# Split weights kept in DRAM after the first token block: one paired load in place of a load, a cast and a subtraction

## The chip, the cores and the metric

The kernel runs on one core of a Trainium2 chip. The metric is the device time of one execution in microseconds (us). Engines: PE (TensorE; PEld is its weight load), DVE (VectorE), ACT (ScalarE), POOL (GpSimd) and SP (SyncE), which here issues every DMA. All DMAs of the core run on the same 16 DMA engines.

## The reference

One decoder layer on x of 2048 tokens by 1024 channels, in float32:

```python
h = _rmsnorm(x, norm_w[l])
proj = h @ w_in[l]                      # 1024 x 8456 columns
(a_q, a_f, a_i, a_g, b_qkv, b_z, b_beta, b_a,
 c_q, c_k, c_v, c_g, gate_logits) = jnp.split(proj, split_points, axis=-1)
y_a = _hgrn2_branch(...)                # gated linear recurrence, 4 heads
y_b = _gated_deltanet_branch(...)       # delta rule, 4 heads
y_c = _swa_sink_branch(...)             # sliding-window attention
ys = jnp.stack([y_a, y_b, y_c], axis=2)
lifted = jnp.einsum('bsnc,ncd->bsnd', ys, w_branch[l])
merged = jnp.sum(jax.nn.sigmoid(gate_logits...) * lifted, axis=2)
x = x + merged @ w_out[l]
return _rmsnorm(x, final_norm)
```

## The kernel before

The 2048 tokens are worked off in four blocks of 512 (`block(s)`). Each block runs through all the weights once: the projections of channel-major outputs (`wct`, through `proj_ct`), of token-major ones (`wtc`, through `proj_v`), the lifts (`wb`, through `merge`) and the output projection (`wo`, through `output`).

To get float32 precision out of products in the type float32r, each matrix is used as a high and a low part, and each product is three matmuls: high by high, high by low, low by high (lines 80 to 82 and 148 to 150). `load_w` (lines 62 to 70) brings one weight tile of 128 partitions by up to 512 columns: a DMA on SP into `wraw` (256 KB; 162 KB for the 324 columns of `wtc`), a cast on ACT into `wh` (line 68) and a subtraction on DVE into `wl` (line 69). A block uses 178 tiles, and `load_w` is called anew for each in each block, 712 times in all. A tile of 512 columns feeds 12 matmuls of 512 columns.

`wraw`, `wh` and `wl` have `WB` = 4 buffers each. So up to four raw tiles can lie loaded and up to four split ones can lie ready; `wraw` becomes free when the subtraction has read it, `wh` and `wl` when the PE has read them.

Beside the projections, `unit_a`, `unit_b` and `unit_c` do the three branches head by head, in chains of small matmuls and of DVE, ACT and POOL work. `unit_b` passes through DRAM several times, one DMA after another: lines 536 (`scrN<-NS`), 539 (`L<-scrN`), 547 (`scrX<-L`) and 549 (`XB<-scrX`). In the first block `bias_c` also writes a table of 1.5 MB (line 261, `scr<-rw`) and reads it back (line 263). The start, ahead of the first block, makes the `wtc` products from the raw input while x is still arriving (`start`, line 178).

In the last block, the second half of `output` calls `mm_tc` with `step` 4: four tiles at a time are held, and each group of four output rows goes through all four before the next row group.

The order of the instructions on each engine and queue is not that of the source: a planner sets it when the program is built, and each queue then works in that fixed order. `tc.issue_after` ties two places to an order by hand.

Of the kernel before, what the change touches and what calls it, by code (L numbers as in the profile page):

```python
# [11 lines left out]
F32 = mybir.dt.float32  # L12
F32R = mybir.dt.float32r
# [3 lines left out]
ALU = mybir.AluOpType  # L17
# [3 lines left out]
P = 128  # L21
# [10 lines left out]
WB = 4  # L32
# [6 lines left out]
def _trunk(tc, S, a, out):  # L39
    nc = tc.nc  # L40
# [4 lines left out]
    sb = ctx.enter_context(tc.tile_pool(name="sb", bufs=2))  # L45
    ps = ctx.enter_context(tc.tile_pool(name="ps", bufs=4, space=PSUM))
    dram = ctx.enter_context(tc.tile_pool(name="dram", bufs=1, space=DRAM))

    V, A, G, T = nc.vector, nc.scalar, nc.gpsimd, nc.tensor
# [9 lines left out]
    def bank(tag="d", w=None):  # L59
        return ps.tile([P, 512], F32, name="ps_" + tag, tag=tag, bufs=4 if tag == "d" else 2)  # L60

    def load_w(src):
        n = src.shape[-1]
        raw = sb.tile([P, 512], F32, name="wraw", tag="wraw", bufs=WB)
        nc.sync.dma_start(raw[:, :n], src)
        wh = sb.tile([P, 512], F32R, name="wh", tag="wh", bufs=WB)
        wl = sb.tile([P, 512], F32R, name="wl", tag="wl", bufs=WB)
        A.copy(wh[:, :n], raw[:, :n])  # L68
        V.tensor_tensor(wl[:, :n], raw[:, :n], wh[:, :n].bitcast(F32), op=ALU.subtract)  # L69
        return wh[:, :n], wl[:, :n]  # L70

    last_mm, last_act = [None], [None]

    def mm_ct(p, src, rh, rl, nk):
        for q in range(nk // 4):
            wh, wl = load_w(src[q])
            for k4 in range(4):
                kt = 4 * q + k4
                ks = slice(k4 * P, (k4 + 1) * P)
                T.matmul(p, wh[:, ks], rh[kt], start=(kt == 0), stop=False)  # L80
                T.matmul(p, wh[:, ks], rl[kt], start=False, stop=False)  # L81
                last_mm[0] = T.matmul(p, wl[:, ks], rh[kt], start=False, stop=(kt == nk - 1)).ins  # L82
# [53 lines left out]
    def mm_tc(src, n, lh, ll, step=1, each=None, tags=("d", "d", "d", "d")):  # L136
        pj = [bank(t) for t in tags]
        for k0 in range(0, KT, step):
            w = []
            for kt in range(k0, k0 + step):  # L140
                if each:
                    each(kt)
                w.append(load_w(src[kt]))
            for j in range(NT):
                js = slice(j * P, (j + 1) * P)
                for kt in range(k0, k0 + step):
                    wh, wl = w[kt - k0]
                    T.matmul(pj[j][:, :n], lh[kt][:, js], wh, start=(kt == 0), stop=False)  # L148
                    T.matmul(pj[j][:, :n], lh[kt][:, js], wl, start=False, stop=False)  # L149
                    T.matmul(pj[j][:, :n], ll[kt][:, js], wh, start=False, stop=(kt == KT - 1))  # L150
        return pj
# [725 lines left out]
```

## Time and profile before

| | |
|---|---|
| median of 3 runs | 2551.77 us (2550.91 to 2551.85) |
| the profiled execution's own time | 2551.53 us |
| its span | 2549.7 us |
| mean granted clock of PE | 0.987 of full speed |
| DMA | 229.97 MB moved, 90 GB/s mean, 12.88 MB of it written to DRAM |

The span is the profiled part of the execution; 1.8 us of its time lie around it. Times in the views are counted from the span's start. Busy time of PE is modelled: matmuls are pipelined, so that one lasts 0.40 us in the trace while the next starts 0.23 us after it. A view's idle time stands in front of the instruction that ended it, with what released it.

### The profile page before, as it was taken

To read this page: it belongs to the slowest core of one execution; us is meant where nothing else is said; L and a number is where in the kernel's file an instruction comes from. 1 tells how busy PE (TensorE), PEld (TensorE's weight loads), DVE (VectorE), ACT (ScalarE), POOL (GpSimd) and SP (SyncE) were. 2 spreads that over 40 slices of the span, in tenths; PEclk is the share of its full clock that TensorE was granted. 3 is DMA by queue.
4 is the path that set the end of the run, shared out by engine and by line. 5 is a ranking of instruction groups with operands and counts; after the bars stand their busy time and mean duration, and the time that the engine had idled before them with its cause. 6 is when DMAs were issued, how large, how long until landed. Compare 5 with 4: busy or idle time off the path is not lost.

```text
span 2549.7 us, 39021 instructions
## 1 busy us (share of the span) xinstructions
PE 2464.3 (97%) x13658; PEld 1945.7 (76%) x13658; DVE 1487.5 (58%) x3706; ACT 1151.0 (45%) x2806; POOL 472.0 (19%) x821
## 2 busy tenths in 40 slices
PE   8899998999999999899999999989999999998998
PEld 7677776778977777677887777767788787776876
DVE  5566566555467657555536666664554676666443
ACT  6354344343545434435444643443434463444343
POOL 3221111211222201120222311111121221111112
PEclk9999999999999999999999999989999999999999
DMA  7423331224522233122452223212344223221233
GB/s 218 79 90 83 84 89 43 66 83 151 164 67 69 78 84 86 43 77 88 147 151 59 78 80 86 80 35 87 91 127 127 63 78 82 84 74 49 83 108 95
DMA packets 162265, 229.97 MB, mean 90 GB/s; under 512 B 49379, under 2 KB 60548, under 8 KB 162068
## 3 DMA queue, kind: packets, MB, share of 16 engines
q1 hardware_dynamic: 162068, 227.47, 31.3%
q8 instruction: 108, 1.77, 0.3%
q14 instruction: 89, 0.73, 0.1%
HBM read 214.53 MB, written 12.88 MB: 89 GB/s over the span
## 4 chain that ended last, share of the span: by engine, by line
PE 87%; DVE 4%; DMA 4%; ACT 2%; POOL 1%; issue 1%; SPq 0%; POOLq 0%; DVEq 0%; ACTq 0%
PE ps_d L80 21%; PE ps_d L81 21%; PE ps_d L82 20%; PE ps_d L149 3%; PE ps_d L148 3%; PE ps_d L150 3%; PE ps_c L371 2%; PE ps_c L701 2%; DMA wraw<-in_wct_dram 1%; PE ps_c L692 1%; DMA scrX<-L 1%; PE ps_c L516 1%; PE ps_c L570 1%; DMA XB<-scrX 1%; DVE wl L69 1%
## 5 line engine op out<-in xcount | busy, mean ns | idle before, releaser
L80 PE MATMUL ps_d<-hH,wh 128*128 128x512 f32 x1952 | 790.8, 405 | 12.3 <-DVE mm L669 5.9
L82 PE MATMUL ps_d<-hH,wl 128*128 128x512 f32 x1952 | 796.4, 408 | 0.1
L68 ACT CAST wh<-wraw 128x512 fp32r<-128x512 f32 (+1 forms) x712 | 429.1, 604 | 812.5 <-PE ps_d L81 659.1
L81 PE MATMUL ps_d<-hL,wh 128*128 128x512 f32 x1952 | 792.0, 406 | 0.0
L69 DVE TENSOR_TENSOR wl<-wraw,wh 128x512 fp32r<-128x512 f32 (+1 forms) x712 | 487.9, 687 | 409.8 <-ACT wh L68 400.0
L80 PEld LDWEIGHTS ps_d<-hH,wh 128*128 128x128 f32 x1952 | 370.9, 190 | 93.2 <-DVE mm L669 6.5
L82 PEld LDWEIGHTS ps_d<-hH,wl 128*128 128x128 f32 x1952 | 370.9, 190 | 79.2 <-issue 1.7
L81 PEld LDWEIGHTS ps_d<-hL,wh 128*128 128x128 f32 x1952 | 370.7, 190 | 79.0 <-issue 0.9
L331 POOL TENSOR_TENSOR msum<-msum,gth 128x512 f32<-128x512 f32 x64 | 104.7, 1638 | 452.1 <-DVE gth L330 452.1
L80 PE MATMUL ps_d<-yH,wh 128*128 128x512 f32 x384 | 154.8, 405 | 3.9 <-ACT yH L311 3.3
L81 PE MATMUL ps_d<-yL,wh 128*128 128x512 f32 x384 | 158.0, 412 | 0.5 <-DVE yL L312 0.5
L82 PE MATMUL ps_d<-yH,wl 128*128 128x512 f32 x384 | 158.1, 412 | 0.0
L148 PE MATMUL ps_d<-wh,mH 128*128 128x512 f32 x256 | 100.1, 391 | 0.0
L149 PE MATMUL ps_d<-wl,mH 128*128 128x512 f32 x256 | 100.0, 391 | 0.0
L150 PE MATMUL ps_d<-wh,mL 128*128 128x512 f32 x256 | 99.9, 390 | 0.0
L471 DVE SCALAR_TENSOR_TENSOR qkB<-raw,convw,qkB 128x512 f32<-128x512 f32 x96 | 71.6, 746 | 29.2 <-ACT qkB L469 28.4
L80 PEld LDWEIGHTS ps_d<-yH,wh 128*128 128x128 f32 x384 | 72.5, 190 | 20.8 <-ACT yH L311 4.1
L81 PEld LDWEIGHTS ps_d<-yL,wh 128*128 128x128 f32 x384 | 73.1, 190 | 19.1 <-DVE yL L312 2.3
L82 PEld LDWEIGHTS ps_d<-yH,wl 128*128 128x128 f32 x384 | 73.1, 190 | 15.3 <-issue 0.3
L330 DVE SCALAR_TENSOR_TENSOR gth<-gth,ps_d 128x512 f32<-128x512 f32 x64 | 43.7, 685 | 68.0 <-PE ps_d L82 67.8
L371 PEld LDWEIGHTS ps_c<-qk 128*64 128x64 f32 x1536 | 53.3, 139 | 38.8 <-issue 20.5
L221 POOL TENSOR_TENSOR soB<-soB,eq 128x1 f32<-128x1 f32 x64 | 15.1, 236 | 346.4 <-ACT junkB L618 346.3
(281 smaller groups left out, 3813.1 us busy)
## 6 DMA issues: line engine op xcount, KB each, us to landing
wraw<-in_wct_dram SPq DMA_DIRECT2D x488, 256.0 KB, 2.6
wraw<-in_wb_dram SPq DMA_DIRECT2D x96, 256.0 KB, 2.6
wraw<-in_wo_dram SPq DMA_DIRECT2D x64, 256.0 KB, 2.6
wraw<-in_wtc_dram SPq DMA_DIRECT2D x64, 162.0 KB, 2.8
xT<-in_xT_dram SPq DMA_DIRECT2D x32, 256.0 KB, 4.2
xs<-in_x_dram SPq DMA_DIRECT2D x32, 256.0 KB, 4.2
rt<-in_x_dram SPq DMA_DIRECT2D x32, 256.0 KB, 3.3
out_dram<-rt SPq DMA_DIRECT2D x32, 256.0 KB, 2.6
```

Of the source, the lines that this page charges most:

```text
L68: A.copy(wh[:, :n], raw[:, :n])
L69: V.tensor_tensor(wl[:, :n], raw[:, :n], wh[:, :n].bitcast(F32), op=ALU.subtract)
L80: T.matmul(p, wh[:, ks], rh[kt], start=(kt == 0), stop=False)
L81: T.matmul(p, wh[:, ks], rl[kt], start=False, stop=False)
L82: last_mm[0] = T.matmul(p, wl[:, ks], rh[kt], start=False, stop=(kt == nk - 1)).ins
L148: T.matmul(pj[j][:, :n], lh[kt][:, js], wh, start=(kt == 0), stop=False)
L149: T.matmul(pj[j][:, :n], lh[kt][:, js], wl, start=False, stop=False)
L150: T.matmul(pj[j][:, :n], ll[kt][:, js], wh, start=False, stop=(kt == KT - 1))
L331: G.tensor_tensor(m, m, th, op=ALU.add)
L371: T.matmul(sp[g * 64:g * 64 + 64, c * 32:(c + 1) * 32], K[:, c * P + g * 64:c * P + g * 64 + 64], qv[:, c, g * nb // 2:(g + 1) * nb // 2, ...
L471: V.scalar_tensor_tensor(dst, raw[:, j:j + TB], convw[:, ti, j:j + 1], dst, op0=ALU.mult, op1=ALU.add)
L701: T.matmul(ob[hh * 64:hh * 64 + 64, ci * P:(ci + 1) * P], cv_[:, c + b, hh * 64:hh * 64 + 64], pts[ci][:, hh, b, :], start=(b == b0), stop ...
```

## The change

In the first block `load_w` does as before, but into one tile `wHL` that holds both parts, and a second DMA then stores the pair (512 KB) in a DRAM tile of its own. The three later blocks find the weight's address in `kept` and load the pair with one DMA of 512 KB; the cast and the subtraction are not done again. `wHL` has 4 buffers, `wraw` 4 as before, and together they take as much SBUF as the three sets of buffers did.

```diff
+    kept = {}
+
     def load_w(src):
         n = src.shape[-1]
-        raw = sb.tile([P, 512], F32, name="wraw", tag="wraw", bufs=WB)
-        nc.sync.dma_start(raw[:, :n], src)
-        wh = sb.tile([P, 512], F32R, name="wh", tag="wh", bufs=WB)
-        wl = sb.tile([P, 512], F32R, name="wl", tag="wl", bufs=WB)
-        A.copy(wh[:, :n], raw[:, :n])
-        V.tensor_tensor(wl[:, :n], raw[:, :n], wh[:, :n].bitcast(F32), op=ALU.subtract)
-        return wh[:, :n], wl[:, :n]
+        key = (src.tensor.name, src.offset)
+        w = sb.tile([P, 2, 512], F32R, name="wHL", tag="wHL", bufs=WB)
+        if key in kept:
+            nc.sync.dma_start(w[:, :, :n].bitcast(F32), kept[key])
+        else:
+            raw = sb.tile([P, 512], F32, name="wraw", tag="wraw", bufs=WB)
+            nc.sync.dma_start(raw[:, :n], src)
+            A.copy(w[:, 0, :n], raw[:, :n])
+            V.tensor_tensor(w[:, 1, :n], raw[:, :n], w[:, 0, :n].bitcast(F32), op=ALU.subtract)
+            kept[key] = dram.tile([P, 2, n], F32, name="kept%d" % len(kept), tag="kept%d" % len(kept))
+            nc.sync.dma_start(kept[key], w[:, :, :n].bitcast(F32))
+        return w[:, 0, :n], w[:, 1, :n]
```

## Rows read from the trace of the kernel before

**Rows 1.** Part 1 of the page: busy time, share, instructions of each engine.

```profile
PE 2464.3 (97%) x13658; PEld 1945.7 (76%) x13658; DVE 1487.5 (58%) x3706; ACT 1151.0 (45%) x2806; POOL 472.0 (19%) x821
```

**Rows 2.** Part 4 of the page: the chain that ended last, by engine.

```profile
PE 87%; DVE 4%; DMA 4%; ACT 2%; POOL 1%; issue 1%; SPq 0%; POOLq 0%; DVEq 0%; ACTq 0%
```

**Rows 3.** Part 5 of the page: the cast and the subtraction of `load_w`.

```profile
L68 ACT CAST wh<-wraw 128x512 fp32r<-128x512 f32 (+1 forms) x712 | 429.1, 604 | 812.5 <-PE ps_d L81 659.1
L69 DVE TENSOR_TENSOR wl<-wraw,wh 128x512 fp32r<-128x512 f32 (+1 forms) x712 | 487.9, 687 | 409.8 <-ACT wh L68 400.0
```

**Rows 4.** Waits of the SP queue: who waited for whom, us, times, longest.

```profile
SPq L65 <- DVE wl L69: 1473.0, 533, 12.3
```

**Rows 5.** ACT over time in the last half output: start, us, what.

```profile
2504.12 0.62 ACT L68 CAST wh<-wraw 128x512 fp32r<-128x512 f32 x1 [2.18 <-PE ps_d L150]
2506.92 0.62 ACT L68 CAST wh<-wraw 128x512 fp32r<-128x512 f32 x1 [2.18 <-PE ps_d L150]
...
2526.92 2.68 ACT L68 CAST wh<-wraw 128x512 fp32r<-128x512 f32 x4 [6.36 <-PE ps_d L150]
```

**Rows 6.** Windows: stretch, its length, engines' busy us, PE clock, DMA share, GB/s.

```profile
0.00:62.00 62.00, 49.90 (x260) 45.06 (x261) 32.86 (x65) 39.66 (x86) 17.98 (x44) 0.97 0.72 223
47.00:52.00 5.00, 4.86 (x23) 3.78 (x22) 3.63 (x13) 3.04 (x9) 0.37 (x2) 1.00 0.98 359
125.00:130.00 5.00, 3.70 (x9) 2.69 (x10) 2.72 (x4) 2.48 (x4) 0.00 (x0) 0.66 0.93 311
560.00:690.00 130.00, 129.98 (x643) 110.36 (x642) 60.59 (x99) 56.97 (x118) 28.01 (x33) 1.00 0.50 154
1290.00:1318.00 28.00, 27.69 (x182) 26.92 (x181) 10.77 (x20) 16.98 (x46) 7.57 (x18) 1.00 0.74 223
690.00:1318.00 628.00, 614.72 (x3421) 485.61 (x3420) 369.90 (x923) 285.88 (x700) 116.21 (x200) 0.99 0.31 89
```

**Rows 7.** Pieces of the chain of waits at lines 68 and 69, second block.

```profile
852.79 0.36 DVE wl L69
...
1091.78 2.84 DVE wl L69 x2
...
1311.80 0.51 DVE wl L69
```

**Rows 8.** DMA issues by line: count, KB each, median us from issue to landing.

```profile
wraw<-in_wct_dram SPq DMA_DIRECT2D x488, 256.0 KB, 2.6
...
wraw<-in_wtc_dram SPq DMA_DIRECT2D x64, 162.0 KB, 2.8
...
scrN<-NS SPq DMA_DIRECT2D x32, 64.0 KB, 2.2
XB<-scrX SPq DMA_DIRECT2D x32, 64.0 KB, 2.3
```

**Rows 9.** The chain in the second block's end: pieces of loading x.

```profile
1297.12 4.04 DMA xs<-in_x_dram
...
1305.90 4.71 DMA xs<-in_x_dram
```

**Rows 10.** The chain of waits in the first block, at a `unit_b`.

```profile
223.60 2.63 DMA scrX<-L
...
226.91 2.36 DMA XB<-scrX
```

**Rows 11.** The chain of waits in the first block, around `scr<-rw`.

```profile
94.30 31.31 DMA wraw<-in_wct_dram
...
126.30 0.60 PE ps_d L80
```

**Rows 12.** The SP queue over time in the first block, at a `unit_b`.

```profile
203.69 1.34 SPq L536 DMA_DIRECT2D scrN<-NS  x2
205.14 0.54 SPq L65 DMA_DIRECT2D wraw<-in_wct_dram  x1
206.64 0.34 SPq L539 DMA_DIRECT2D L<-scrN  x1
```

## The prediction

> **What bounds the kernel now.** First the busy time of each engine: PE 97%, DVE 58%, ACT 45% [rows 1]. Then the chain that ended last: 87% of it is PE, DVE and ACT together 6%, DMA 4% [rows 2]. So the kernel is bound by PE, and an edit gains only where it takes away a wait of PE. Third, what the change removes: 712 casts of 604 ns and 712 subtractions of 687 ns [rows 3]. ACT sat idle 812.5 us ahead of its casts, 659.1 of them until PE had read the buffer that was to be written over. The cast thus runs when PE frees a buffer, three tiles ahead of its use, and is late for nobody. SP tells the same: 1473 us of its waiting, in 533 pieces, is for a subtraction to free `wraw` [rows 4]. A raw load is therefore issued about seven tiles ahead of its use: four raw tiles and three split ones.
>
> How long a tile lasts on PE: in the last `output` the casts, paced by PE, start at 2504.12 and 2506.92 [rows 5], so 2.8 us for 12 matmuls of 512 columns, and 2.8 x 324/512 = 1.8 us for a `wtc` tile. The second block lasts 628 us [rows 6], 3.5 us for each of its 178 tiles with all other work.
>
> Last the DMAs, which the change makes larger: the windows show what 16 engines deliver when they are full, 311 GB/s at a share of 0.93 and 359 at 0.98 [rows 6].
>
> **The change, part by part.**
>
> *Relief of ACT and DVE.* 534 casts x 604 ns = 323 us and 534 subtractions x 687 ns = 367 us go, all in blocks 2 to 4. DVE falls to about 1121 us (44%), ACT to 828 (32%). That is hidden work but for the pieces that stand on the chain. In the second block there are 14 such pieces of lines 68 and 69, the first at 852.79, the last at 1311.80; their sum is 6.8 us, and the largest is two subtractions in 2.84 us at 1091.78 [rows 7]. Three blocks at that rate give 20 us. Behind each removed piece stands the next releaser of the same PE instruction, so I take half, a gain of 10. Bounds: 0, and 30, if shorter queues on DVE and ACT also let the planner set a better order.
>
> The two subtractions of 2.84 us are twice as long as two of 687 ns [rows 3, 7]. [...]
>
> *The pair's loads in blocks 2 to 4.* A 256 KB load lands in 2.6 us [rows 8]; the second 262 KB at 359 GB/s add 0.7, so 3.3 for the pair. A pair can only be issued when PE has read the buffer's old tile, so its lead is three tiles, not seven: 3 x 2.8 = 8.4 us, and the 3.3 hide behind these matmuls. Two places have less cover.
>
> (a) `proj_v` between blocks: 3 x 1.8 = 5.4 us of lead, while loads of x next to it took 4.0 to 4.7 us [rows 9]. The 28 us there have DMA busy 0.74 of the time [rows 6], 20.7 us; 16 tiles x 166 KB more are 2.7 MB, 7.4 us at 359 GB/s, which makes 28.1 of 28. I take a loss of 2 us at each of two boundaries, 4 in all; bounds 0 and 10.
>
> (b) The last half `output` with its four tiles held: the last four casts start at 2526.92, as PE frees the buffers, 0.67 us apart, and 0.62 + 0.69 us later a tile is ready [rows 5]. In their place come four pair loads that are issued then: 0.3 us of issue and 3.3 to land, 2.3 later than before, and then 524 KB / 359 GB/s = 1.46 us apart, 3 x 0.8 = 2.4 more. That is 4.7 us; nothing follows that could take it back. I take 4; bounds 0 (the planner orders the matmuls by tile) and 6 (the first four tiles too).
>
> Small DMAs on the chain, `scrX<-L` 2.63 and `XB<-scrX` 2.36 us [rows 10], stand behind loads that take 0.7 us longer: two such DMAs, two units, three blocks, half the time: 12 x 0.35 = 4, of which half has cover. I take 2; bounds 0 and 4.
>
> *The stores in the first block.* 178 more DMAs, each for its subtraction's end. On SP a store and the raw load four tiles later wait for the same subtraction, so the wait itself is no new one, and what stands behind it on SP, the transfers of `unit_b` and the loads of x, waits as it does now. The buffer of a pair is free again only when its store has landed, about 9 us after the split: three tiles. Then 786 KB go with each tile, 281 GB/s in a dense stretch of 2.8 us a tile, against 311 to 359 [rows 6]: hidden, but with 10 to 20% to spare and nothing for other traffic. So I go through the stretches where there is other traffic.
>
> (c) Start, 0 to 62 us: DMA busy 0.72 x 62 = 44.6 us [rows 6]. Stores of 16 `wtc` tiles x 332 KB and some five of 524 KB are 7.9 MB, 22 us more, 66.6 in all: 5 over, and unevenly spread, ahead of the loads that PE waits for. I take 8; bounds 0 and 22.
>
> (d) `scr<-rw`: a weight load issued at 94.30 lands 31.31 us later, behind that transfer, and PE goes on at 126.30 [rows 11]. The stores of the tiles split meanwhile stand in the same rings. Four of them are 2.1 MB or 6.7 us at 311 GB/s, in the window of a share of 0.93 [rows 6]. I take 3; bounds 0 and 7.
>
> (e) `unit_b`: each unit sends four small DMAs one after the other, 2.2 to 2.6 us each [rows 8, 10]; each may stand behind a store, 1.46 us. At half the time, 4 x 0.73 = 2.9 a unit, two of four units on the chain, 5 in all; bounds 0 and 12.
>
> (f) 560 to 690 us, the third `merge`, `output` and the next `proj_v`: busy 0.50 x 130 = 65 us [rows 6]. 40 stores are 21 MB or 58 us, the larger `wtc` loads 7 more: 130 of 130. I take 3; bounds 0 and 12.
>
> [...]
>
> **Sum.** -10 + 4 + 4 + 2 + 8 + 3 + 5 + 3 = +19 us, on the profiled execution's 2551.5 (span 2549.7 and 1.8 around it; the median of 2551.8 is 0.2 above it): 2570.5, so 2570, 0.7% slower.
>
> **The rivals.**
>
> *Faster: the transfers are hidden.* DMA is busy 0.31 of the second block [rows 6]; stores can lie in its gaps. Then (c) to (f) fall to 3 or so, the relief is the 20 us of the chain, and (a), (b) and the small DMAs cost about 4: 2551.5 - 20 + 7 = 2538. It decides itself at whether the first block loses less than the 15 us or so that the others gain. Against it: the full windows at the start and end of that block.
>
> *No change.* The two sides meet within 5 us, which is about what can be told from no change (0.2%): 2547 to 2556.
>
> *Much slower: the first block runs at the pace of its transfers.* No row shows loads and stores of this size mixed. If they get 200 GB/s, a tile takes 3.93 us instead of 3.53: 0.4 x 178 = 71 more, about 2620. It decides at 786 KB / 3.53 us = 223 GB/s.
>
> *Much slower: the queue keeps the order of the source.* Then each raw load waits behind the store of the tile before, for its split: 2.6 + 0.6 + 0.7 + 0.3 = 4.2 us a tile, 0.7 x 178 = 125 more, about 2670. Against it: SP issued a weight load at 205.14 between lines 536 and 539, between which the source has none [rows 12].
>
> That the later blocks don't find their pairs can be left aside: the address in the key is the same in each block and another one for each tile.
>
> **How the numbers follow.** Forecast 0.52 (its own range 2557 to 2595), faster 0.25, no change 0.11, pace of transfers 0.08, order of the source 0.04. So faster 0.25, same 0.11, slower 0.64. The range that leaves out the lower part of the faster case and the two much slower ones goes from 2536 (relief of 30, costs of 15) to 2605 (costs near 60, relief of 6).
>
> **What would show it.** Lines 68 and 69 with 178 instructions each; 534 loads of 512 KB landing in 3 to 4 us; the first block longer by some 20 us, with DMA shares near 1 at its start and its end; the later blocks shorter by about 3 each; PE idle at the last half `output`. The prediction is wrong if the first block's PE idle hardly grows, or if the later blocks gain over 7 us each because the order was set anew, or if PE waits for pairs in the middle of these blocks.

## The result, and the profile after

The changed kernel takes 2531.9 us (median; 2529.7 to 2537.9) against 2551.3 us before: ratio 0.9927, 95% interval 0.9911 to 0.9943, 0.73% faster. The forecast was 2570, so the sign was wrong, and the time also lies below the low end of the range, 2536. The execution profiled is the slowest of the four (2537.9, span 2536.1), so the two traces differ by 13.7 us where the medians differ by 19.4.

The groups that answer to [rows 3] and [rows 8], and the busy row of PE that answers to [rows 1]:

```profile
PE 2434.0 (96%) x13658; PEld 1944.4 (77%) x13658; DVE 1167.5 (46%) x3172; ACT 863.7 (34%) x2272; POOL 435.8 (17%) x821
...
L74 DVE TENSOR_TENSOR wHL<-wraw,wHL 128x512 fp32r<-128x512 f32 (+1 forms) x178 | 122.0, 688 | 81.8 <-ACT wHL L73 79.4
...
L73 ACT CAST wHL<-wraw 128x512 fp32r<-128x512 f32 (+1 forms) x178 | 106.7, 602 | 134.3 <-PE ps_d L89 83.5
...
wHL<-kept SPq DMA_DIRECT2D x486, 512.0 KB, 3.6
kept<-wHL SPq DMA_DIRECT2D x162, 512.0 KB, 4.1
...
wHL<-kept SPq DMA_DIRECT2D x48, 324.0 KB, 3.9
```

Casts and subtractions are down to 178 each, the 534 pair loads are there and land in 3.6 to 3.9 us; the change did what it says. To see where the time went, both executions are cut at the first sigmoid of each block (`F`, line 347 before, 354 after). The columns are those of [rows 6]: stretch, its length, busy time of PE, PEld, DVE, ACT and POOL, granted clock, DMA share, GB/s. First the kernel before: start, first block, and blocks 2 to 4 together.

```profile
0.00:59.41 59.41, 47.31 (x249) 42.97 (x250) 32.86 (x65) 37.08 (x82) 17.33 (x42) 0.97 0.71 220
59.41:698.73 639.32, 615.45 (x3383) 484.45 (x3383) 369.45 (x923) 284.25 (x700) 116.29 (x202) 0.98 0.34 94
...
698.73:2549.74 1851.01, 1801.51 (x10029) 1418.29 (x10027) 1085.20 (x2718) 829.70 (x2025) 338.42 (x577) 0.99 0.30 85
```

The same of the changed kernel:

```profile
0.00:62.42 62.42, 43.47 (x232) 40.09 (x233) 32.26 (x64) 33.31 (x69) 14.69 (x39) 0.95 0.80 257
62.42:713.33 650.91, 612.92 (x3393) 487.85 (x3392) 359.15 (x902) 279.19 (x691) 120.69 (x205) 0.97 0.69 230
...
713.33:2536.07 1822.74, 1777.58 (x10036) 1416.43 (x10034) 776.06 (x2206) 551.18 (x1513) 300.46 (x577) 0.99 0.50 159
```

Subtract PE's busy time from the length, and the two parts come apart:

| | PE idle before | after | difference | PE busy before | after | difference |
|---|---|---|---|---|---|---|
| start and first block | 36.0 | 56.9 | +20.9 | 662.8 | 656.4 | -6.4 |
| blocks 2 to 4 | 49.5 | 45.2 | -4.3 | 1801.5 | 1777.6 | -23.9 |
| sum | 85.5 | 102.1 | +16.6 | 2464.3 | 2434.0 | -30.3 |

PE waits 16.6 us more, close to the +19 that the prediction added up (a match that is partly luck, as `e2_two_tiles` shows below). It came out faster because PE is busy 30.3 us less, with the same matmuls. One uninterrupted run of projection matmuls of the second block shows it, first and last two of 84 rows before:

```profile
979.71 0.39 PE L81 MATMUL ps_d<-hL,wh 128*128 128x512 f32 x1
979.95 0.39 PE L82 MATMUL ps_d<-hH,wl 128*128 128x512 f32 x1
...
998.85 0.39 PE L82 MATMUL ps_d<-hH,wl 128*128 128x512 f32 x1
999.08 0.40 PE L80 MATMUL ps_d<-hH,wh 128*128 128x512 f32 x1
```

and of 88 rows after:

```profile
959.75 0.39 PE L89 MATMUL ps_d<-hH,wHL 128*128 128x512 f32 x1
959.98 0.39 PE L87 MATMUL ps_d<-hH,wHL 128*128 128x512 f32 x1
...
979.25 0.39 PE L88 MATMUL ps_d<-hL,wHL 128*128 128x512 f32 x1
979.47 0.40 PE L89 MATMUL ps_d<-hH,wHL 128*128 128x512 f32 x1
```

19.37 us over 83 steps are 233.4 ns from start to start; 19.72 over 87 are 226.7. Over all consecutive 512-column pairs of the trace (steps of 215 to 245 ns, so those at the full clock) the projections and lifts step by 233.3 ns before and 227.7 after; what lies above 226 ns sums to 43.0 us in 6482 pairs before and 14.6 us in 6545 after. That difference, 28.4 us, is nearly the whole 30.3.

What differs is where the operands lie. Addresses in each partition, in bytes, as the built programs have them:

```
                 moving: hH, hL        yH, yL            stationary: high and low parts of w
before           16,512 to 49,279      49,280 to 65,663   129,728 to 180,927   (2 KB tiles)
after            16,512 to 49,279      49,280 to 65,663    82,048 to  98,431   (4 KB tiles)
```

The addresses fall into groups by size, the largest lowest, so the paired tile of 4 KB went below the groups of 2 KB. (One tile of the 712 of the kernel before lies lower, at 65,664.) In the output projection `w` is the moving operand and `mH`, `mL` the stationary one, and there the steps went the other way: 228.0 ns before, 232.2 after.

### The profile page after: what moved, and what is told of

It is laid out like the page before. It is cut to its first block, busy times and chain, and to the rows that moved or that the text cites. A ratio compares the mean times of both kernels' runs of the same rounds, so it can differ in the third digit from the quotient of the medians.

```text
span 2536.1 us, 37457 instructions
## 1 busy us (share of the span) xinstructions
PE 2434.0 (96%) x13658; PEld 1944.4 (77%) x13658; DVE 1167.5 (46%) x3172; ACT 863.7 (34%) x2272; POOL 435.8 (17%) x821
## 5 line engine op out<-in xcount | busy, mean ns | idle before, releaser
L87 PE MATMUL ps_d<-hH,wHL 128*128 128x512 f32 x1952 | 785.1, 402 | 20.9 <-ACT wHL L73 15.4
L88 PE MATMUL ps_d<-hL,wHL 128*128 128x512 f32 x1952 | 783.1, 401 | 0.0
L89 PE MATMUL ps_d<-hH,wHL 128*128 128x512 f32 x1952 | 779.0, 399 | 0.0
L87 PEld LDWEIGHTS ps_d<-hH,wHL 128*128 128x128 f32 x1952 | 369.1, 189 | 95.2 <-ACT wHL L73 15.8
L89 PEld LDWEIGHTS ps_d<-hH,wHL 128*128 128x128 f32 x1952 | 368.4, 189 | 71.1 <-issue 1.9
L88 PEld LDWEIGHTS ps_d<-hL,wHL 128*128 128x128 f32 x1952 | 369.0, 189 | 67.9 <-issue 1.5
L74 DVE TENSOR_TENSOR wHL<-wraw,wHL 128x512 fp32r<-128x512 f32 (+1 forms) x178 | 122.0, 688 | 81.8 <-ACT wHL L73 79.4
L87 PE MATMUL ps_d<-yH,wHL 128*128 128x512 f32 x384 | 153.6, 402 | 6.2 <-ACT yH L318 4.1
L89 PE MATMUL ps_d<-yH,wHL 128*128 128x512 f32 x384 | 153.5, 400 | 0.0
L88 PE MATMUL ps_d<-yL,wHL 128*128 128x512 f32 x384 | 152.5, 397 | 0.1
L73 ACT CAST wHL<-wraw 128x512 fp32r<-128x512 f32 (+1 forms) x178 | 106.7, 602 | 134.3 <-PE ps_d L89 83.5
L155 PE MATMUL ps_d<-wHL,mH 128*128 128x512 f32 x256 | 100.9, 395 | 1.9 <-DMA wHL<-kept 1.9
L156 PE MATMUL ps_d<-wHL,mH 128*128 128x512 f32 x256 | 100.9, 394 | 0.0
L87 PEld LDWEIGHTS ps_d<-yH,wHL 128*128 128x128 f32 x384 | 72.2, 189 | 22.0 <-ACT yH L318 4.9
L89 PEld LDWEIGHTS ps_d<-yH,wHL 128*128 128x128 f32 x384 | 72.6, 189 | 14.7 <-issue 0.3
L378 PEld LDWEIGHTS ps_c<-qk 128*64 128x64 f32 x1536 | 52.7, 137 | 33.3 <-issue 23.3
```

The source lines that it names most:

```text
L73: A.copy(w[:, 0, :n], raw[:, :n])
L74: V.tensor_tensor(w[:, 1, :n], raw[:, :n], w[:, 0, :n].bitcast(F32), op=ALU.subtract)
L378: T.matmul(sp[g * 64:g * 64 + 64, c * 32:(c + 1) * 32], K[:, c * P + g * 64:c * P + g * 64 + 64], qv[:, c, g * nb // 2:(g + 1) * nb // 2, ...
```

## The experiments

Ratios are against the kernel before, run on the same chip between the others (medians 2548 to 2552 us). "PE idle" and "PE busy" are those of blocks 2 to 4, from window rows like the above. Every edit also lets the planner write a new order, so no two kernels differ by the edit alone; that is why the theories are tried in several ways.

**Place and relief, by four combinations.** Theory A: place; theory B: relief of VectorE and ScalarE. First, the split in every block, but into the paired tile (`e1_pair_always`):

```diff
+        w = sb.tile([P, 2, 512], F32R, name="wHL", tag="wHL", bufs=WB)
-        wh = sb.tile([P, 512], F32R, name="wh", tag="wh", bufs=WB)
-        wl = sb.tile([P, 512], F32R, name="wl", tag="wl", bufs=WB)
```

> The kernel before with one change: high and low part stand in one tile wHL of 4 KB per partition, split in every block as before; nothing is stored or loaded as a pair. In the program built from it, wHL lies at bytes 82048 to 98431 of each partition, where the changed kernel has it (before: wh and wl between 129728 and 180927). Theory A (place): most of the gain of the changed kernel comes from the place of the weight tiles. In the trace of before, consecutive 512-column matmuls of the projections start 233 ns apart (6,482 undisturbed pairs of all stages lie 43.0 us above 226 ns each), in the changed kernel 227 to 228 (14.6 us above). So this kernel should show 227 to 228 ns and about 28 us less: 2523 (2516 to 2531). Theory B (relief): the gain comes from the casts and subtractions that are gone; they are all here, so the time stays at 2551 (2546 to 2558), and the spacing of 233 ns should stay as ACT and DVE work as much as before.

Measured: 2559.8 us, ratio 1.0036 (1.0020 to 1.0053). The steps fell to 227.8 ns, as theory A has it, but the time rose: a miss for both. Then the reverse, the kept pair in two 2 KB tiles that lie at 129,728 and up, each stored and loaded by its own DMA (`e2_two_tiles`):

```diff
-        w = sb.tile([P, 2, 512], F32R, name="wHL", tag="wHL", bufs=WB)
+        wh = sb.tile([P, 512], F32R, name="wh", tag="wh", bufs=WB)
+        wl = sb.tile([P, 512], F32R, name="wl", tag="wl", bufs=WB)
...
-            nc.sync.dma_start(w[:, :, :n].bitcast(F32), kept[key])
+            for k, t in enumerate((wh, wl)):
+                nc.sync.dma_start(t[:, :n].bitcast(F32), kept[key][:, k, :])
```

> The changed kernel with the pair in two tiles of 2 KB per partition, wh and wl, stored and loaded with two DMAs of 256 KB each; splits in the first block only, as in the changed kernel. In the program built from it, wh and wl lie at 129728 to 180927, as before the change. Theory A (place): spacing of the projections' matmuls 233 ns again, and about 28 us more than the changed kernel's 2532: 2560 (2550 to 2570), which is slower than before. Theory B (relief): ACT and DVE are as free as in the changed kernel, the bytes are the same, and 712 more DMAs hide on SP: 2532 (2525 to 2540).

Measured: 2548.3 us, ratio 0.9977 (0.9960 to 0.9994), steps 233.2 ns as before; the time lies between the two theories and in the range of neither. Its blocks 2 to 4:

```profile
705.58:2546.31 1840.73, 1800.03 (x10036) 1418.59 (x10034) 775.74 (x2206) 551.20 (x1513) 298.33 (x577) 0.99 0.49 157
```

Busy as before (1800.0 against 1801.5), idle 40.7 against 49.5: the change without the better place relieves PE by 8.8 us in these blocks. The start and first block last 6.9 us longer than before (705.6 against 698.7), with 8.1 us more of PE idle (44.1 against 36.0). So at the old pace the change comes out 3.6 us faster by the medians, and PE's idle time hardly moves in all: -0.7 us, where the prediction had +19. Does it lose to the changed kernel by its place or by its 534 more loads? (The expectations speak of 482; the traces have 1068 loads of 256 or 162 KB against 534 of pairs.) `e12_two_dmas` keeps the paired tile where it was and loads it by two DMAs:

```diff
-            nc.sync.dma_start(w[:, :, :n].bitcast(F32), kept[key])
+            for k in range(2):
+                nc.sync.dma_start(w[:, k, :n].bitcast(F32), kept[key][:, k, :])
```

> The changed kernel, its pair tile where it was (bytes 82,048 to 98,431 of each partition), but each kept pair loaded by two transfers of 256 KB. This parts the two edits of the run with two tiles high up in SBUF, which was 16 us slower than the changed kernel. Theory P (that run lost by the place alone, its spacing of 233.2 ns against 227.7): the time stays within 5 us of the changed kernel's, 2527 to 2537 us, ratio to before 0.990 to 0.995. Theory D (it lost by the 482 more transfers in SyncE's queue): most of the 16 us is here too, 2542 to 2549 us.

Measured: 2533.7 us, ratio 0.9923 (0.9897 to 0.9948), steps 227.7 ns: place, not the number of loads. Next, place alone, with the parts released one by one as before (`e5_before_low`):

```diff
+    whs = const.tile([P, WB, 512], F32R, name="wh", tag="wh")
+    wls = const.tile([P, WB, 512], F32R, name="wl", tag="wl")
...
+        wh = whs[:, nw_[0] % WB, :]
+        wl = wls[:, nw_[0] % WB, :]
```

> The kernel before, with no other edit than that the high parts and the low parts lie in two resident arrays of four slots at bytes 57,472 to 73,856 of each partition (the kernel before has them at 129,728 to 180,927), used in turn; casts, subtractions and loads are all there, and each slot is released by its own last reader. Theory P (much of what the change gave comes from where the pair lies): the spacing of consecutive 512-column products of the projections falls from 233.3 to about 227.7 ns, and the time falls by 8 to 25 us, to 2527 to 2544 us, ratio 0.990 to 0.997. Theory W (what the change gave is the work taken from VectorE and ScalarE in blocks 2 to 4; the place is worth nothing in time): the spacing may fall, but waits elsewhere take it up, ratio 0.998 to 1.003, as in the run in which a joint tile was split in every block (1.0036).

Measured: 2578.6 us (median of six runs that scatter from 2563.3 to 2612.2, more than any other kernel here), ratio 1.0102 (1.0058 to 1.0147, without the longest run), a miss for both. The steps at the full clock are 227.8 ns, yet the trace has a mean granted clock of 0.962, against 0.987 before. A part of the third block shows why (columns as above):

```profile
1715.00:1720.00 5.00, 4.06 (x17) 2.79 (x17) 2.18 (x7) 0.61 (x2) 0.00 (x0) 0.59 0.00 0
1720.00:1725.00 5.00, 4.02 (x19) 2.91 (x19) 1.67 (x5) 1.30 (x6) 0.75 (x2) 0.50 0.01 3
1725.00:1730.00 5.00, 3.67 (x13) 2.79 (x14) 1.25 (x4) 1.46 (x6) 0.74 (x2) 0.50 0.00 2
1730.00:1735.00 5.00, 4.45 (x19) 3.89 (x19) 1.24 (x4) 1.06 (x4) 2.18 (x6) 0.50 0.01 2
```

PE has run out of projections there and is left with the chains of a delta-rule head, idle for 0.55 to 1.33 us of each 5; its granted clock is 0.50 from 1720 to 1735 us. Summed over blocks 2 to 4, the trace has a clock of 0.50 for 37 us before and in the changed kernel, 42 in `e2_two_tiles`, 83 in `e1_pair_always`, 153 here.

Last, the removed work put back beside the changed kernel, in blocks 2 to 4 (`e9_work_back`); nothing reads its result:

```diff
             nc.sync.dma_start(w[:, :, :n].bitcast(F32), kept[key])
+            junk = sb.tile([P, 512], F32, name="wjunk", tag="wraw", bufs=WB)
+            A.copy(junk[:, :n].bitcast(F32R), w[:, 0, :n].bitcast(F32))
+            V.tensor_tensor(junk[:, :n].bitcast(F32R), w[:, 1, :n].bitcast(F32), junk[:, :n], op=ALU.subtract)
```

> The changed kernel, with the removed work put back beside it: in blocks 2 to 4 ScalarE copies the high part of each loaded pair and VectorE subtracts, both into a tile that nothing reads (482 of each; the pair itself is loaded as in the changed kernel, so the products wait for nothing of it except when a slot is freed). Theory R (the 28 us that blocks 2 to 4 gave come from the relief of VectorE and ScalarE): blocks 2 to 4 go back to 625 us and more, and the time rises by 15 to 28 us from the changed kernel, to 2547 to 2560 us. Theory P (they come from the place of the pair in SBUF, which keeps two of them on one side of it): the time stays within 6 us of the changed kernel's, 2526 to 2538 us.

Measured: 2581.0 us, ratio 1.0127 (1.0108 to 1.0146), 49 us above the changed kernel and more than theory R asked for. The edit adds more than it puts back: the pair's buffer is now also held until the copy and the subtraction have read it. Its blocks 2 to 4:

```profile
715.16:2581.04 1865.88, 1793.53 (x10030) 1427.51 (x10028) 1110.83 (x2720) 840.96 (x2027) 337.81 (x577) 0.98 0.49 155
```

Blocks 2 to 4 of the four combinations, and of the kernels that repeat one:

| split work in blocks 2 to 4 | pair high in SBUF, 233 ns | pair low, 228 ns |
|---|---|---|
| done | before: 1851.0 (idle 49.5) | `e1` 1863.0 (66.4), `e5` 1884.4 (57.2), `e9` 1865.9 (72.4) |
| not done | `e2`: 1840.7 (40.7) | after: 1822.7 (45.2), `e12` 1821.2 (43.4) |

With the pair high, leaving out the split work gives 10 us; with the pair low, 40 and more. The shorter steps are worth 18 us without the split work and less than nothing with it. So neither theory holds alone: taken as it stands, the table gives 10 us for relief alone, nothing for the shorter steps alone, and 28 for both. But the rows of the slow kernels do not show VectorE or ScalarE short of time for the split work. In `e9`, VectorE stands idle ahead of the added subtraction, which waits for the added copy, and that for the pair's load; the chain of `unit_b` waits behind it (VectorE, then PE):

```profile
2276.71 0.69 DVE L72 TENSOR_TENSOR wjunk<-wHL,wjunk 128x512 fp32r<-128x512 f32 x1 [4.10 <-ACT wjunk L71]
2278.37 0.45 PE L570 MATMUL ps_c<-X,NS 128*64 128x64 f32 x8 [2.36 <-DVE X L560]
```

Such idle time of VectorE sums to 359 us in `e9`, so this run holds up the chains in a way that the kernel before did not. In `e1` the same step waits for the last of `unit_b`'s DMAs:

```profile
1622.29 0.44 DVE L549 STREAM_TRANSPOSE X<-XB 64x256 f32<-64x256 f32 x1 [4.16 <-DMA XB<-scrX]
1623.46 0.70 PE L559 MATMUL ps_c<-X,NS 128*64 128x64 f32 x8 [3.31 <-DVE X L549]
```

The changed kernel waits longer for these DMAs (35.6 us of VectorE's idle time in blocks 2 to 4, against 18.9 in `e1`), yet PE stops there for 1.2 us at most, since it has other matmuls in that place. The clock differs as well: it is 0.50 for 83 us of these blocks in `e1` and in `e9`, for 37 in the changed kernel. So the runs show what the place is worth without the split work (`e2` against the changed kernel and `e12`). Whether with the split work it fails for want of relief, or only because the planner's orders leave PE nothing to do at these stops, is not shown.

**The first block.** `e3_one_store` leaves out all but one store for each width, so that blocks 2 to 4 load one and the same pair for all weights of a width.

```diff
+            if n not in one:
+                one[n] = dram.tile([P, 2, n], F32, name="kept%d" % n, tag="kept%d" % n)
+                nc.sync.dma_start(one[n], w[:, :, :n].bitcast(F32))
+            kept[key] = one[n]
```

> The changed kernel with one store for each width instead of 178; all later pair loads read that one pair in DRAM, so blocks 2 to 4 compute with a wrong weight (this part of the computation is changed; the loads, their sizes and all other work are the same). What the stores cost: from the first unit's start in each block, the first block lasts 650.9 us in the changed kernel against 639.3 before, and the start 3.0 more, while 10 us of it should have been won by the closer matmuls. Theory A: the stores cost that, 15 us or so, mostly at the one stop of PE of 15.4 us behind the table write; without them about 2515 (2508 to 2522). Theory B: the stop is the table write's alone and the stores are hidden: 2530 (2526 to 2536).

Measured: 2518.95 us, ratio 0.9868 (0.9842 to 0.9894). Start and first block last 690.8 us against 713.3; the others 1825.3 against 1822.7. The stores cost 13 us by the medians, all of it there.

The largest single stop is at `scr<-rw`. Before, PE waited 4.1 us there and went on at 126.30 [rows 11]. In the changed kernel, over time, SP and then PE:

```profile
92.34 0.30 SPq L268 DMA_DIRECT2D scr<-rw  x1
92.69 9.77 SPq L72 DMA_DIRECT2D wraw<-in_wct_dram  x1
102.51 4.34 SPq L53 DMA_DIRECT2D norma<-in_norma_dram  x1
106.95 4.30 SPq L76 DMA_DIRECT2D kept<-wHL  x1
```

```profile
111.62 0.39 PE L89 MATMUL ps_d<-hH,wHL 128*128 128x512 f32 x1
127.43 0.80 PE L87 MATMUL ps_d<-hH,wHL 128*128 128x512 f32 x1 [15.42 <-ACT wHL L73]
```

Issues that otherwise take 0.3 to 0.5 us take 4 to 10 here; in the kernel before, four raw loads in the same place took 20.3 us. PE goes on about as long after the table's issue in these kernels: 34.2 us after it before, 35.1 in the changed kernel, 35.0 in `e2`, 34.3 in `e3`, which has no stores there. What differs is how long its work lasts until it stops: 30.0, 19.7, 27.3 and 30.3 us, or the 512-column matmuls of about 7, 5, 6 and 7 weight tiles. So the stores lengthen the stop by leaving PE fewer tiles that are ready, not by putting off its end. Three ways out were tried. By head, eight DMAs from one partition each (`e4_bias_by_head`):

```diff
-        nc.sync.dma_start(scr.rearrange("p h w -> h p w"), rw.rearrange("h (o w) -> h o w", o=1).broadcast_to([8, P, RW]))
+        for hd in range(8):
+            nc.sync.dma_start(scr[:, hd, :].rearrange("(o p) w -> o p w", o=1),
+                              rw[hd:hd + 1, :].rearrange("h (o w) -> h o w", o=1).broadcast_to([1, P, RW]))
```

> The changed kernel, with the table write of the first block (1.5 MB in one DMA whose source has 8 partitions) made as 8 DMAs of 192 KB, one for each head, each broadcast over 128 rows. In the trace of the changed kernel PE stops for 15.4 us up to 127.4 us, with the DMA share at 0.45 to 0.64: half the engines carry the table. Theory A: the table write keeps half of the 16 engines and the queue, and weight loads and stores wait behind it; by head it spreads over all engines, the stop shrinks to under 4 us, and the time falls by 10 to 14: 2519 (2514 to 2525). Theory B: the stop comes from the number of bytes in flight there, stores included, and stays: 2532 (2527 to 2537).

Measured: 2564.6 us, ratio 1.0050 (1.0034 to 1.0066); SP was busy 41 us issuing the eight, and PE stopped for 39.8. From ScalarE's queue (`e6_bias_act`, `nc.scalar.dma_start` in place of `nc.sync.dma_start` in that line):

> The changed kernel, with the one transfer scr<-rw (L268) issued from ScalarE's queue and not from SyncE's. Theory Q (the weight loads behind it are held back because SyncE's queue is slow to pass while the 1024 rows of that transfer are being issued): loads pass it, the TensorE stop of 15.4 us up to 127.4 us falls under 8 us, and the time falls by 5 to 12 us from the changed kernel, to 2520 to 2527 us. Theory X (the transfer itself takes the DMA engines that the loads need, whichever queue issues it): the stop stays above 12 us and the time within 3 us of the changed kernel's.

Measured: 2547.4 us, ratio 0.9987 (0.9973 to 1.0001), 15 us slower than the changed kernel; the longest stop of PE grew to 27.6 us, with SP issuing nothing from 91 to 125 us. Theory Q falls; of theory X the stop holds, but not the unchanged time. Read from 128 partitions (`e10_bias_wide`, and the same edit on the kernel before, `e11_before_bias_wide`):

```diff
+        for hd in range(8):
+            if hd % 4 == 0:
+                relw = sb.tile([33, 4, P], F32, name="relw", tag="w%d" % (5 + hd // 2))
+                G.tensor_copy(relw, relb[:, hd:hd + 4].rearrange("p (h o) -> p h o", o=1).broadcast_to([33, 4, P]))
+            pb = bank("c%d" % (hd % 2))
+            T.matmul(pb[:, :RW], relw[:, hd % 4, :], onehot, start=True, stop=True)
+            rw = sb.tile([P, RW], F32, name="rw", tag="tr", bufs=2)
+            V.tensor_scalar(rw, pb[:, :RW], 8.0, None, op0=ALU.mult)
+            nc.sync.dma_start(scr[:, hd, :], rw)
```

> The changed kernel, with the one transfer scr<-rw from 8 partitions (1024 rows of 1536 bytes) made as eight transfers from 128 partitions each: TensorE forms each head's row on all 128 partitions (eight small products), VectorE scales it, and each row of DRAM then comes from a partition of its own. Bytes and rows are the same. Theory N (that transfer is slow because it reads only 8 partitions, and its time holds up the weight loads): the TensorE stop of 15.4 us before 127.4 us falls under 6 us and the time falls by 8 to 14 us from the changed kernel, to 2518 to 2524 us. Theory X (1.5 MB more in that stretch stops the loads however it is read): the stop stays above 10 us, and the time within 4 us of the changed kernel's.

> The same edit on the kernel before, whose stop there was 4.1 us. Theory N: a gain of 2 to 5 us, 2545 to 2548 us, so that the changed kernel with this edit stays some 25 us ahead of it. Theory X: no change within 3 us.

One window of each, at 8, 1 and 128 source partitions (the changed kernel, `e4`, `e10`):

```profile
115.00:120.00 5.00, 0.00 (x0) 0.00 (x0) 0.00 (x0) 0.00 (x0) 0.00 (x0) 0.65 0.56 76
```

```profile
115.00:120.00 5.00, 0.00 (x0) 0.00 (x0) 0.00 (x0) 0.00 (x0) 0.00 (x0) 0.68 0.86 27
```

```profile
100.00:105.00 5.00, 5.00 (x18) 3.06 (x18) 1.72 (x3) 0.62 (x1) 0.31 (x1) 1.00 0.82 295
```

From 8 partitions the 16 DMA engines are busy for 0.56 of the time in the mean and 76 GB/s go through; from one partition they are busy for 0.86 and 27 GB/s go through; from 128 there are 295 GB/s, other transfers included, and PE does not stop. The share is a mean over the 16 engines: how many of them carry the table is not shown. `e11` took 2537.9 us, ratio 0.9956 (0.9939 to 0.9973), a gain of 10 where 2 to 5 were expected. In `e10` the stop is gone and start and first block last 700.0 us, 13.4 less; but the median, 2532.3 us, ratio 0.9930 (0.9909 to 0.9950), is that of the changed kernel: theory N has the stop right and the time wrong, theory X the reverse. Of the 13.4 us, 8.1 are lost again in blocks 2 to 4 (1830.9 us against 1822.7), most of it in the last, which took 595.5 us against 589.4; and the trace of the changed kernel is 6.0 us above its median, that of `e10` 0.3. In the last block:

```profile
2230.12 0.39 PE L87 MATMUL ps_d<-hH,wHL 128*128 128x512 f32 x1
2232.59 0.45 PE L571 MATMUL ps_c<-X,NS 128*64 128x64 f32 x8 [2.08 <-DVE X L561]
...
2235.67 0.63 PE L87 MATMUL ps_d<-hH,wHL 128*128 128x512 f32 x1
2236.10 0.63 PE L88 MATMUL ps_d<-hL,wHL 128*128 128x512 f32 x1
```

Just after a stop of 2.08 us the clock is at 0.50 for 6.8 us, from 2234.7 on, and steps are 0.43 us. With half of these 6.8 us lost, an estimate, the stop and the clock together cost 5.5 us. The changed kernel has no such fall of the clock in this block before 2304 us. Why the other order made PE stop there is not shown.

**The stores' queue.** `e7_store_pool` issues the stores from GpSimd (`nc.gpsimd.dma_start` in line 76):

> The changed kernel, with the 178 stores of the pair issued from GpSimd's queue and not from SyncE's. Leaving the stores out gave 13 us (2518.95 against 2531.9). Theory O (a store costs by its place in SyncE's order: it waits for the subtraction, and the loads behind it wait with it): 8 to 13 us come back, 2519 to 2524 us. Theory T (the stores cost by their 47 MB on the DMA engines): the time stays within 4 us of the changed kernel's.

Measured: 2560.4 us, ratio 1.0046 (1.0030 to 1.0062), a miss for both theories: start and first block take 732.4 us. The stop at the table is shorter there, 11.0 us, but the start takes 68.5 us instead of 62.4, and in the first block PE stops for 7.0, 3.1 and 6.2 us for `X` (line 557, in `unit_b`), where the changed kernel never stops for more than 1.2. GpSimd, too, works in a fixed order, and where a store stands in it, it waits for the subtraction, 193 us in all:

```profile
129.04 1.94 POOL L401 TENSOR_TENSOR tots<-tots 128x128 f32<-128x128 f32 x6
140.88 1.84 POOL L76 DMA_DIRECT2D kept<-wHL  x3 [9.90 <-DVE wHL L74]
```

At the three stops VectorE itself waits for `unit_b`'s last DMA (`XB<-scrX`), for 7.3, 2.9 and 7.2 us. What makes it late there is not shown.

`e13_late_store` is `e10_bias_wide` without the stores of the start's 16 tiles, which are split again in block 2 and stored there:

```diff
+            nsplit[0] += 1
+            if nsplit[0] > 16:
+                kept[key] = dram.tile([P, 2, n], F32, name="kept%d" % len(kept), tag="kept%d" % len(kept))
+                nc.sync.dma_start(kept[key], w[:, :, :n].bitcast(F32))
```

> The changed kernel with the bias rows read from 128 partitions, and without the stores of the first 16 tiles of the start: those are split again in block 2, stored there, and loaded as pairs in blocks 3 and 4 only. Theory S (the start's loss is that its stores stand between its loads in SyncE's queue): the start falls from 57.0 to some 53 us, as in the kernel before with the same bias edit (53.2), and the time by 3 to 4 us from 2532.3, to 2528 to 2530 us. Theory E (what it saves there it gives back as 16 casts and subtractions at the beginning of block 2): within 2 us of 2532.3.

Measured: 2517.3 us, ratio 0.9863 (0.9831 to 0.9895), 15 us below `e10` where theory S gave 3 to 4, and the fastest kernel here: 33 us ahead of the kernel before. The start is 50.0 us against 57.0, the first block 637.8 against 643.0, the rest 1825.8 against 1830.9. Theory S named the start alone; why the other two gained as well is not shown.

**The tail.** `e8_tail` takes one tile at a time in the last half `output` as well:

```diff
-                pj = mm_tc(a["wo"][half], 512, mH, mL, 4 if half and s == NSB - 1 else 1)
+                pj = mm_tc(a["wo"][half], 512, mH, mL, 1)
```

> The changed kernel, with one weight tile at a time in the last half of the last output and not four (step 1 there as elsewhere). Theory L (that half waits for a group of four 512 KB loads at its two steps, as the landing of 5.3 us at the end of the chain of waits showed): the stretch from the last but one to the last output addition falls from 21.5 to 15 to 17 us, and the time by 4 to 6 us, to 2526 to 2528 us. Theory M (the four were taken together so that the first three rows of output can be finished ahead of the last): the stretch gains but the additions at the end come all at once, and the time stays within 2 us.

Measured: 2535.7 us, ratio 0.9939 (0.9915 to 0.9963). The stretch between the additions is 22.0 us, not shorter than the 21.5 of the changed kernel; theory L falls. Theory M expected a shorter stretch and an unchanged time, and the time is 3.8 us longer.

## Why the prediction was wrong, point by point

*The step that failed* is the one that fixed how long a tile lasts on PE, "so 2.8 us for 12 matmuls of 512 columns", and let PE's busy time stand as it was in both kernels. The change moved the split parts of the weights to other addresses, and by that a tile went from 2.80 to 2.73 us (`e5`, which moves them low and does all of the split work, steps by 227.8 ns; `e2`, which leaves them high without it, by 233.2). No term of the sum stood for it; it is the -30.3 us of PE busy. The trace before held both spacings, 233 ns in the projections and 228 on average in the output projection; I read one place, from 2504 to 2507 us, where the steps are 233 because the parts of `mH` and `mL` used there lie low (86,144 to 104,576), and took it for a constant of the instruction.

*The sum of the waits* was wrong too at the pace that it assumed. `e2`, which keeps that pace, is the nearest to what I forecast, though its pairs are loaded in two parts: the start and first block have 8.1 us more of PE idle where (c) to (f) gave 19, and blocks 2 to 4 have 8.8 less where relief, (a), (b) and the small DMAs added up to 0. So 2570 would have been too high without the new place as well, and the 16.6 us of the changed kernel come close to 19 partly because a faster PE runs into waits that the slower one did not.

*Relief* (-10; bounds 0 and 30). With the place as before, `e2` has 8.8 us less of PE idle in blocks 2 to 4, and 4.2 us of its idle time are new waits for pairs: the relief itself was some 13 us, an estimate. It also came another way than the working has it: in blocks 2 to 4 of the kernel before PE nowhere waits for a cast or a subtraction, and what fell were its waits on VectorE in the heads' chains (`X`, `qs` and `E`, from 17.5 to 6.7 us). With the pair low, the kernels that do the split work take 40 us longer in these blocks (`e1`, `e9`); how much of that is the split work itself and how much the order is not shown.

*(c) the start* (+8): its PE idle rose by 6.9 us, from 12.1 to 19.0. The size was right, the way was not: the DMA engines were not full, at a share of 0.80 from 0 to 62 us. `e13`, without these stores, has a start of 50.0 us where `e10` has 57.0. *(d)* `scr<-rw` (+3, bounds 0 and 7): the stop grew from 4.1 to 15.4 us, 11.3. Mis-sized and outside the bounds: I counted the bytes of the stores that stand in the queue, which put off its end by some 1 us, and not the tiles that PE would lack, by which it stopped some 10 us earlier after the table's issue. *(e)* and *(f)* (+5, +3): the rest of the first block lost some 3 us (14.1 of PE idle less the 11.3), so these were too high. In (f)'s stretch, 560 to 690 us, the DMA share was 0.81 and PE idle 0.3 us; even where DMA was fullest, PE had no wait:

```profile
600.00:640.00 40.00, 40.00 (x177) 32.95 (x176) 20.39 (x32) 16.95 (x29) 8.76 (x5) 1.00 0.91 324
```

*(a) `proj_v`* (+4): all of PE's waits for a kept pair sum to 5.3 us over the whole execution; this holds the boundaries and part of the tail. *(b) the tail* (+4, bounds 0 and 6): from the last but one to the last half's first addition 15.3 us before and 21.5 after, +6.2, with a load on the chain of waits. First before, then after, then that load:

```profile
2516.47 2.48 DVE L719 TENSOR_TENSOR rt<-ps_d,rt 128x512 f32<-128x512 f32 x4
2531.74 0.69 DVE L719 TENSOR_TENSOR rt<-ps_d,rt 128x512 f32<-128x512 f32 x1 [1.42 <-PE ps_d L150]
```

```profile
2498.98 2.76 DVE L726 TENSOR_TENSOR rt<-ps_d,rt 128x512 f32<-128x512 f32 x4 [16.32 <-PE ps_d L157]
2520.47 1.39 DVE L726 TENSOR_TENSOR rt<-ps_d,rt 128x512 f32<-128x512 f32 x2 [18.73 <-PE ps_d L157]
```

```profile
2510.85 5.32 DMA wHL<-kept
```

Some of it comes back: from the last but one half's first addition to the end of the span it is 33.3 us before and 37.1 after, +3.8, so the size of 4 was right. That the four tiles at a time cause the 6.2 is not borne out: `e8` has 22.0 us in the same stretch without them.

*The rivals.* The faster one named a point that decides, "whether the first block loses less than the 15 us or so that the others gain", and by that it came out: 14.6 us lost, 28.3 gained. But its mechanism, hidden transfers, is not what made the changed kernel faster: PE's idle time still grew by 16.6 us. The two much slower ones are out: the first block is 12 us longer, not 71 or 125. Of the signs that I had named for being wrong, later blocks that gain over 7 us each showed in two of the three (10.1, 12.4, 5.8), with another cause than the one given there. For the rate of full DMA engines I took 359 GB/s. The changed kernel moves more, at the beginning and at the end of its first block (a share above 1 comes of counting a packet where it starts):

```profile
60.00:70.00 10.00, 10.00 (x45) 8.26 (x45) 3.09 (x5) 7.80 (x14) 4.65 (x9) 1.00 1.03 390
650.00:655.00 5.00, 5.00 (x23) 4.05 (x22) 3.02 (x5) 2.28 (x6) 0.90 (x1) 1.00 1.04 416
```

So 359 is not the most that the engines deliver here, and the times of (c) and (f), worked out with it, came out too long.

*What stays open:* why the lower place slows the kernel more in `e5` than in `e1`, since the planner wrote another order for each; how the gain of relief splits between order and engine time, since no two kernels here have the same order; and, for the same reason, how exact the 10 and 18 us of the table are, and whether the shorter steps need the relief.

## What to carry to other kernels

Split a time difference into the busy and the idle time of the bounding engine before looking for a cause: here the sum of the waits looked much as forecast, and the gain was in the pace of matmuls that nobody had edited. Then hold that pace fixed in a run of its own (`e2`) before calling the rest of the sum right. A change of a tile's shape moved it in SBUF here, from 129,728 and up to 82,048, and the pace of its matmuls went with it (233.3 to 227.7 ns in the projections, 228.0 to 232.2 in the output projection), so measure the spacing of the same instruction in both traces. A gain of pace is not yet a gain of time: the kernels with the shorter steps and all of the split work (`e1`, `e5`) were slower than the kernel before, with more idle time of PE in blocks 2 to 4 (66.4 and 57.2 us against 49.5) and more time at a clock of 0.50 (83 and 153 us against 37). And look at what stands in front of each stop before calling an engine late: work put back beside a kernel (`e9`) can hold it up in a way that the removed work did not.

## What was not expected of the hardware

In the kernels here, consecutive float32r matmuls of 512 columns step by 226 to 228 ns where the moving and the stationary operand both lie low or both lie high in a partition, and by 232 to 234 ns where one is low and one is high. In the projections the moving one is always low (16,512 to 65,663, in `e5` up to 82,047), and the steps were 233.3 and 233.2 ns with the weights at 129,728 and up (before, `e2`, `e11`), 227.7 to 227.8 with them below 98,432 (after, `e1`, `e5`, `e9`, `e10`, `e12`, `e13`). In the output projection, with `mH` and `mL` mostly at 107,136 and above, it is the reverse: 228.0 and 227.6 with the weights high, 232.0 to 232.8 with them low. By single tiles of `mH` and `mL` that a step leads to, the kernel before, with its weights high, has 230.5 to 232.4 ns for those that begin at 104,576 or below, 228.8 to 230.1 from 107,136 to 113,344, and 226.5 to 227.2 for nearly all from 117,440 up. The changed kernel, with its weights low, still has 227 to 229 ns for those up to 114,816, 231.5 at 123,520, and 232 to 234 for nearly all from 127,680 up. So the change is not a sharp line: tiles that begin between some 105,000 and 125,000 bytes lie in between, and the runs do not show what in the chip it is.

A granted clock of 0.50 is met here just after a stop of 2.08 us (`e10`, above) and, from 1720 to 1735 us of `e5`, in chains of small matmuls in which PE is idle for 0.55 to 1.33 us of each 5 (above). What sets it is not shown.
